# Rounding x on another engine, splitting the loads over two queues, and multiplying the first two row pairs plainly

## The chip, the cores and the metric

The kernel runs on one core of a Trainium2 chip. The metric is the device time of one execution in microseconds (us). Before the change it is 456.4 us, the median of three runs (455.51 to 456.47).

## What is computed

The inputs are `x` of 16 x 512 x 768 and `w_qkv` of 768 x 2304, both float32. The reference is one matrix product, cut into three parts:

```python
qkv = np.matmul(x, w_qkv)
q = qkv[..., :hidden]
k = qkv[..., hidden:2*hidden]
v = qkv[..., 2*hidden:]
return np.stack([q, k, v], axis=0).astype(np.float32)
```

`x` has 8192 rows. All of `x`, `w_qkv` and the output pass through the DMA queues once: 25.2 MB and 7.1 MB in, 75.5 MB out.

## The kernel before

The rows of `x` are taken in 32 pairs `p` of 2 x 128 rows. The 2304 columns of `w_qkv` are three regions: two quads `q` of 1024 columns, each of two blocks of `CB` = 512, and between them 256 remaining columns. The 768 terms of the sum are six steps of 128 (`KT`), or two halves of three (`KH`).

A pair times a quad is a 2 x 2 by 2 x 2 block product. It is done with seven block products in place of eight, and sums of blocks stand in for the eighth. Products 1 and 2 take x rounded to bf16 (tile `xb`) and w rounded to bf16 (`b11`, `b21`). Products 3 to 7 take sums of blocks of x (tile `s`, five slots) and sums of blocks of w (tiles `t1` to `t4`, and `b22`) in float32. Each product is three matmuls of 128 x 512 on PE (TensorE), at L155. `do(u, n)` issues product n of quad u and what takes its result out of PSUM: ACT (ScalarE) copies at L169, L176, L182 and L186, DVE (VectorE) adds at L173, L183 and L189. Product 1 opens PSUM tile `u.x`; products 6, 7 and 4 add into the same tile, so each of them can begin only when the ACT copy of the state before it has been read out. Products 5 and 3 share `u.y` in the same way. `rem(p)` multiplies a pair by the 256 remaining columns in bf16 (12 matmuls, L207, taken out by DVE at L212).

`two(a, b, fill, between)` interleaves two quads on PE, in the order a1, b1, a2, a6, b2, b6, a5, a7, b5, b7, a4, b4, then `rem`, then a3, b3. From pair 3 on, one call does both quads of one pair, and this is the loop: 29 calls.

Inside `two`, behind a5, stands `between()`. It calls `prep(p + 1)`: DVE transposes the next pair's x from `xin` to `xf` (L116), ACT rounds it to `xb` (L123) and copies one block into `s` (L125), and POOL (GpSimd) makes the four sums of `s` (L127 to L130). Then the load of pair p + 3 is issued. Engines work their instructions in the order of the program text; nothing is reordered.

All w loads and the x loads from pair 3 on are issued by SP (SyncE) in one queue, and so are all stores. The x loads of pairs 0 to 2 are issued by ACT. Every load of a tile is four DMAs of 32 partitions each (0 to 31, 32 to 63, 64 to 95, 96 to 127). At the start pairs 0 to 2 are prepared and their `rem` done, then w's quad 0 is rounded and summed, and the first `two` does quad 0 of pairs 0 and 1.

Of the kernel before, what the change touches and what calls it, by code (L numbers as in the profile page):

```python
# [9 lines left out]
def kernel(  # L10
# [20 lines left out]
    nc = tc.nc  # L31
    P = 128
# [5 lines left out]
    KT = K // P  # L38
    KH = KT // 2
# [45 lines left out]
    def load_block(q, h, c):  # L85
        t = big_pool.tile([P, KH, CB], fp32, name="st", tag="big")
        load_w(t, h * KH, KH, Q_OFF[q] + c * CB, CB)
        stage[q, h, c] = t

    def casts_w(q, which):  # L90
        if which == 0:
            nc.scalar.activation(b11[q][:], stage[q, 0, 0][:], ident)
            nc.scalar.activation(b21[q][:], stage[q, 1, 0][:], ident)
        else:
            nc.scalar.activation(b22[q][:], stage[q, 1, 1][:], ident)

    def sums_w(q):
        t1, t2, t3, t4 = ts[q]
        v = nc.vector
        v.tensor_tensor(t1[:], stage[q, 0, 1][:], stage[q, 0, 0][:], op=sub)  # L100
        v.tensor_tensor(t2[:], stage[q, 1, 1][:], t1[:], op=sub)
        v.tensor_tensor(t3[:], stage[q, 1, 1][:], stage[q, 0, 1][:], op=sub)
        v.tensor_tensor(t4[:], stage[q, 1, 0][:], t2[:], op=sub)

    xin, xf, xb, sr = {}, {}, {}, {}

    def load_x(p, eng):
        t = xin_pool.tile([P, 2 * P // G, KC], fp32, name="xin")
        rows = x_flat[p * 2 * P:(p + 1) * 2 * P, :].rearrange("(g b) k -> b g k", b=G)
        for i in range(4):  # L110
            eng.dma_start(t[i * G:(i + 1) * G], rows[:, :, i * KC:(i + 1) * KC])
        xin[p] = t

    def prep(p):
        t = xf_pool.tile([P, KT, 2 * P], fp32, name="xf")
# [28 lines left out]
    def product(u, n, ps, start, stop):  # L144
        b, s = xb[u.p], sr[u.p]
        t1, t2, t3, t4 = ts[u.q]
        if n == 1:
            lhs, rhs = [b[:, j, :P] for j in range(KH)], b11[u.q]
        elif n == 2:
            lhs, rhs = [b[:, KH + j, :P] for j in range(KH)], b21[u.q]  # L150
# [12 lines left out]
    def do(u, n):  # L163
        c11, c12 = u.o[:, 0, :CB], u.o[:, 0, CB:]
        c21, c22 = u.o[:, 1, :CB], u.o[:, 1, CB:]
        if n == 1:
            u.x = bank()
            product(u, 1, u.x, True, True)
            nc.scalar.activation(c11, u.x[:], ident)  # L169
        elif n == 2:  # L170
            u.z = bank()
            product(u, 2, u.z, True, True)
            nc.vector.tensor_tensor(c11, c11, u.z[:], op=add)  # L173
        elif n == 6:
            product(u, 6, u.x, False, True)
            nc.scalar.activation(c12, u.x[:], ident)  # L176
        elif n == 5:
            u.y = bank()
            product(u, 5, u.y, True, True)
        elif n == 7:  # L180
            product(u, 7, u.x, False, True)
            nc.scalar.activation(c22, u.x[:], ident)  # L182
            nc.vector.tensor_tensor(c22, c22, u.y[:], op=add)  # L183
        elif n == 4:
            product(u, 4, u.x, False, True)
            nc.scalar.activation(c21, u.x[:], ident)  # L186
# [52 lines left out]
    load_x(0, nc.scalar)  # L239
    load_x(1, nc.scalar)  # L240
    st_rem = big_pool.tile([P, KT, REM], fp32, name="st", tag="big")
    load_w(st_rem, 0, KT, R_OFF, REM)
    for h, c in ((0, 0), (1, 0), (0, 1), (1, 1)):
        load_block(0, h, c)
# [7 lines left out]
    prep(2)
    rem(2)
    casts_w(0, 1)
    sums_w(0)
    a, b = quad(0, 0), quad(1, 0)
    load_block(1, 0, 0)
    load_block(1, 1, 0)

    def rest_of_w():  # L260
        load_block(1, 0, 1)
        load_block(1, 1, 1)
        load_x(3, nc.sync)

    two(a, b, nothing, rest_of_w)
    casts_w(1, 0)
    casts_w(1, 1)
    sums_w(1)
    two(quad(2, 0), quad(0, 1), nothing, lambda: load_x(4, nc.sync))
    prep(3)  # L270
    two(quad(1, 1), quad(2, 1), nothing, lambda: load_x(5, nc.sync))

    for p in range(3, NP):
        a, b = quad(p, 0), quad(p, 1)

        def between():
            if p + 1 < NP:
                prep(p + 1)
            if p + 3 < NP:
                load_x(p + 3, nc.sync)  # L280

        two(a, b, lambda: rem(p), between)


# [28 lines left out]
```

## Time and profile before

| | |
|---|---|
| median of three runs | 456.4 us |
| the profiled execution, its own time | 455.96 us |
| its span, first to last instruction | 454.2 us |
| PE busy (matmul) | 366.0 us, 1728 matmuls |
| DVE, ACT, POOL busy | 219.1, 218.1, 126.6 us |
| moved by DMA | 108.10 MB, mean 238 GB/s |

The engines run beside each other, so the busy times don't add up to the span. 1.8 us of the time lie outside the span. Up to about 84 us the work is the start (w arrives, the first pairs are mixed), from there to 446 us the loop, and the last 8 us store what is left. Line numbers in this document's rows are those of the kernel before.

### The profile page before, as it was taken

The page shows a single profiled execution, that of the slowest core. Times are in us where ns is not written, and L with a number is a line of the kernel's source. Part 1 is how long each engine was busy: PE and PEld are TensorE (multiplying, and loading weights), DVE is VectorE, ACT ScalarE, POOL GpSimd, SP SyncE. Part 2 cuts the span into 40 slices and gives each one's busy share as a digit, 9 for nine tenths or more (in the row PEclk, how much of TensorE's full clock was granted, in tenths as well). Part 3 has the DMA queues.
Part 4 walks back from the last instruction along what each step waited for, and adds up shares of the span by engine and source line. Part 5 has one row for each costly group of instructions (what it writes and reads, how often), then busy time and mean ns, then how long its engine had stood idle before and what let it go on. Part 6 is the DMA issues. An engine that isn't in the chain of part 4 may idle for free.

```text
span 454.2 us, 5237 instructions
## 1 busy us (share of the span) xinstructions
PE 366.0 (81%) x1728; PEld 247.6 (55%) x1728; DVE 219.1 (48%) x264; ACT 218.1 (48%) x328; POOL 126.6 (28%) x132
## 2 busy tenths in 40 slices
PE   0248598888998888888898888888899888888892
PEld 0125265555665566655665556655566556665561
DVE  0328652454554455455455455445455445545542
ACT  0553535555445554554445555555544555455440
POOL 0540003332223333332222333333222333333200
PEclk9999888999999999999999999999999999999997
DMA  9988977787777777887777777788777777785555
GB/s 180 223 197 191 251 250 203 241 269 252 243 253 230 237 234 234 271 278 259 250 253 235 232 238 232 247 279 270 237 259 252 231 237 236 232 270 210 208 210 208
DMA packets 82779, 108.10 MB, mean 238 GB/s; under 512 B 5184, under 2 KB 63296, under 8 KB 82752
## 3 DMA queue, kind: packets, MB, share of 16 engines
q1 hardware_dynamic: 79488, 105.40, 74.9%
q10 hardware_dynamic: 3264, 2.36, 2.6%
q8 instruction: 14, 0.23, 0.2%
q14 instruction: 13, 0.11, 0.1%
HBM read 32.24 MB, written 75.50 MB: 237 GB/s over the span
## 4 chain that ended last, share of the span: by engine, by line
DMA 28%; PE 28%; DVE 21%; issue 12%; ACT 8%; SPq 1%; DVEq 1%; ACTq 0%
DMA out_dram<-o 19%; PE ps L155 19%; DVE xf L116 12%; PE ps L207 9%; DMA xin<-in_x_dram 5%; DVE o L189 4%; DVE orem L212 4%; DMA st<-in_w_qkv_dram 4%; ACT s L125 3%; ACT o L182 3%; ACT xb L123 1%; SPq L78 1%; DVEq L116 1%; DVE o L173 0%; ACT o L169 0%
## 5 line engine op out<-in xcount | busy, mean ns | idle before, releaser
L155 PE MATMUL ps<-t,s 128*128 128x512 f32 x768 | 210.5, 417 | 53.5 <-ACT o L182 43.9
L155 PEld LDWEIGHTS ps<-t,s 128*128 128x128 f32 x768 | 144.0, 191 | 102.4 <-ACT o L182 57.4
L127 POOL TENSOR_TENSOR s<-xf 128x384 fp32r<-128x384 f32 x32 | 32.3, 1009 | 302.9 <-DVE xf L116 302.9
L155 PE MATMUL ps<-b,xb 128*128 128x512 bf16 x384 | 96.4, 387 | 0.0
L183 DVE TENSOR_TENSOR o<-o,ps 128x512 f32<-128x512 f32 x64 | 41.5, 685 | 80.1 <-ACT o L182 80.1
L169 ACT ACTIVATE o<-ps 128x512 f32<-128x512 f32 x64 | 38.0, 596 | 84.9 <-PE ps L155 83.5
L173 DVE TENSOR_TENSOR o<-o,ps 128x512 f32<-128x512 f32 x64 | 43.9, 688 | 62.2 <-ACT o L169 38.6
L207 PE MATMUL ps<-w_rem,xb 128*128 128x256 bf16 x384 | 51.2, 287 | 26.5 <-ACT xb L123 26.5
L123 ACT ACTIVATE xb<-xf 128x1536 bf16<-128x1536 f32 x32 | 47.5, 1484 | 42.7 <-DVE xf L116 42.7
L176 ACT ACTIVATE o<-ps 128x512 f32<-128x512 f32 x64 | 38.2, 598 | 51.6 <-PE ps L155 51.6
L116 DVE STREAM_TRANSPOSE xf<-xin 128x1536 f32<-128x1536 f32 x32 | 56.8, 1774 | 10.9 <-DMA xin<-in_x_dram 10.9
L155 PEld LDWEIGHTS <-xb 128*128 128x128 bf16 x384 | 33.0, 99 | 49.1 <-issue 19.6
L207 PEld LDWEIGHTS <-xb 128*128 128x128 bf16 x384 | 36.6, 102 | 40.5 <-ACT xb L123 27.5
L212 DVE COPY orem<-ps 128x512 f32<-128x512 f32 x32 | 22.1, 692 | 68.2 <-PE ps L207 68.2
L155 PE MATMUL ps<-b,s 128*128 128x512 f32 x192 | 52.1, 406 | 0.0
L186 ACT ACTIVATE o<-ps 128x512 f32<-128x512 f32 x64 | 38.3, 598 | 20.3 <-PE ps L155 17.2
L189 DVE TENSOR_TENSOR o<-o,ps 128x512 f32<-128x512 f32 x64 | 44.0, 687 | 3.5 <-PE ps L155 3.1
L182 ACT ACTIVATE o<-ps 128x512 f32<-128x512 f32 x64 | 34.7, 586 | 7.0 <-PE ps L155 7.0
L155 PEld LDWEIGHTS ps<-b,s 128*128 128x128 f32 x192 | 33.9, 189 | 6.1
L130 POOL TENSOR_TENSOR s<-xf,s 128x384 fp32r<-128x384 f32 x32 | 32.7, 1022 | 0.0
L128 POOL TENSOR_TENSOR s<-s,xf 128x384 fp32r<-128x384 f32 x32 | 31.8, 995 | 2.5
L129 POOL TENSOR_TENSOR s<-xf 128x384 fp32r<-128x384 f32 x32 | 32.5, 1014 | 0.0
(14 smaller groups left out, 42.3 us busy)
## 6 DMA issues: line engine op xcount, KB each, us to landing
out_dram<-o SPq DMA_DIRECT2D x64, 768.0 KB, 4.8
xin<-in_x_dram SPq DMA_DIRECT2D x116, 192.0 KB, 4.0
out_dram<-o SPq DMA_DIRECT2D x64, 256.0 KB, 3.9
out_dram<-orem SPq DMA_DIRECT2D x32, 256.0 KB, 2.2
st<-in_w_qkv_dram SPq DMA_DIRECT2D x36, 192.0 KB, 6.5
xin<-in_x_dram ACTq DMA_DIRECT2D x12, 192.0 KB, 7.1
```

The lines of the kernel that those rows point to most:

```text
L116: nc.vector.transpose(t.rearrange("p j (g b) -> p g j b", b=G), xin.pop(p).rearrange("p g (j a) -> p g j a", a=G),)
L123: nc.scalar.activation(b[:], t[:], ident)
L155: nc.tensor.matmul(ps[:], lhs[j], rhs[:, j, :], start=(start and j == 0), stop=(stop and j == KH - 1), skip_group_check=True,)
L169: nc.scalar.activation(c11, u.x[:], ident)
L173: nc.vector.tensor_tensor(c11, c11, u.z[:], op=add)
L176: nc.scalar.activation(c12, u.x[:], ident)
L182: nc.scalar.activation(c22, u.x[:], ident)
L183: nc.vector.tensor_tensor(c22, c22, u.y[:], op=add)
L186: nc.scalar.activation(c21, u.x[:], ident)
L189: nc.vector.tensor_tensor(c12, c12, u.y[:], op=add)
L207: nc.tensor.matmul(ps[:, r, :], xb[p][:, j, r * P:(r + 1) * P], w_rem[:, j, :], start=(j == 0), stop=(j == KT - 1), skip_group_check=True,)
L212: nc.vector.tensor_copy(out=o[:], in_=ps[:])
```

## The change

- Rounding: x is rounded to bf16 on POOL (`round_x`), and POOL also copies the block into `s`; ACT no longer does either. In the loop, transpose, rounding and sums of pair p + 1 are issued behind b1 of pair p (`early`), not behind a5.
- The result of `rem` is taken out by ACT, not by DVE, and `rem` stands between a4 and b4.
- Loads: of the four DMAs of a tile, those to partitions 0 to 63 are issued by SP, those to 64 to 127 by a second engine, in the order 0, 2, 1, 3. The second engine is POOL for w and for x of pairs 0 to 3, ACT for x from pair 4 on. In the loop the load of pair p + 2 is issued behind b1 of pair p.
- Pairs 0 and 1 are multiplied plainly in bf16, one block of 512 columns at a time as w arrives (`direct`: 24 matmuls for each block and both pairs), 96 matmuls in place of 84. DVE rounds w for it. Then pairs 2 and 3 go through two calls of `two` (quad 0, then quad 1), and the loop begins with pair 4: 30 calls in all.
- w's sums are made one by one between this work; those of quad 1 go into the buffers that w's quad 0 was staged in.

```diff
-    def load_w(dst, j0, nj, off, cols):
-        for i in range(4):
+    def load_w(dst, j0, nj, off, cols, other):
+        for i in (0, 2, 1, 3):
             k0 = i * KC + j0 * G
-            nc.sync.dma_start(
+            eng = nc.sync if i < 2 else other
+            eng.dma_start(
...
-    def load_x(p, eng):
+    def load_x(p, other):
...
-        for i in range(4):
+        for i in (0, 2, 1, 3):
+            eng = nc.sync if i < 2 else other
             eng.dma_start(t[i * G:(i + 1) * G], rows[:, :, i * KC:(i + 1) * KC])
...
-    def prep(p):
+    def transpose(p):
...
+    def round_x(p):
+        xb[p] = xb_pool.tile([P, KT, 2 * P], bf16, name="xb")
+        nc.gpsimd.tensor_copy(out=xb[p][:], in_=xf[p][:])
+
+    def sums_x(p):
...
-        nc.scalar.activation(b[:], t[:], ident)
         s = s_pool.tile([P, 5, KH, P], f32r, name="s")
-        nc.scalar.activation(s[:, 0], a22, ident)
...
+        g.tensor_copy(out=s[:, 0], in_=a22)
...
-        nc.vector.tensor_copy(out=o[:], in_=ps[:])
+        nc.scalar.activation(o[:], ps[:], ident)
...
+    def direct(p, c, o, w):
+        for r in range(2):
+            ps = bank()
+            for j in range(KT):
+                nc.tensor.matmul(
+                    ps[:], xb[p][:, j, r * P:(r + 1) * P], w[:, j, :],
+                    start=(j == 0), stop=(j == KT - 1),
+                )
+            nc.scalar.activation(o[:, r, c * CB:(c + 1) * CB], ps[:], ident)
...
-    def two(a, b, fill, between):
+    def two(a, b, fill, early, mid):
         do(a, 1)
         do(b, 1)
+        early()
         do(a, 2)
         do(a, 6)
         do(b, 2)
         do(b, 6)
         do(a, 5)
-        between()
         do(a, 7)
         do(b, 5)
         do(b, 7)
+        mid()
         do(a, 4)
+        fill()
         do(b, 4)
-        fill()
         do(a, 3)
...
+    w = casts(0, 0)
+    direct(0, 0, o0[0].o, w)
+    direct(1, 0, o0[1].o, w)
+    transpose(2)
+    round_x(2)
+    sums_x(2)
+    load_x(3, gp)
+    w = casts(0, 1)
+    direct(0, 1, o0[0].o, w)
...
+    two(quad(2, 0), quad(3, 0), lambda: rem(2), nothing, nothing)
+    def ahead():
+        transpose(4)
+        round_x(4)
+        sums_x(4)
+    two(quad(2, 1), quad(3, 1), lambda: rem(3), lambda: load_x(5, ac), ahead)
+    for p in range(4, NP):
+        def early():
+            if p + 1 < NP:
+                transpose(p + 1)
+                round_x(p + 1)
+                sums_x(p + 1)
+            if p + 2 < NP:
+                load_x(p + 2, ac)
+        two(quad(p, 0), quad(p, 1), lambda: rem(p), early, nothing)
```

On ACT, one call of the loop before reads as follows; L169, L176, L182 and L186 are the copies behind products 1, 6, 7 and 4, each for quads a and b.

```order
L169 ACTIVATE o<-ps 128x512 x2
L176 ACTIVATE o<-ps 128x512 x2
L123 ACTIVATE xb<-xf 128x1536
L125 ACTIVATE s<-xf 128x384
L182 ACTIVATE o<-ps 128x512 x2
L186 ACTIVATE o<-ps 128x512 x2
```

After the change the same call on ACT is this, with the copies now at L179, L186, L192 and L196, the remaining columns at L222, and two x loads at L115.

```order
L179 ACTIVATE o<-ps 128x512 x2
L115 DMA xin<-in_x_dram 32x8x192 x2
L186 ACTIVATE o<-ps 128x512 x2
L192 ACTIVATE o<-ps 128x512 x2
L196 ACTIVATE o<-ps 128x512
L222 ACTIVATE orem<-ps 128x512
L196 ACTIVATE o<-ps 128x512
```

The two instructions on x between the copies are gone from ACT; two DMA issues and the copy of the remaining columns have come.

On POOL the program after the change begins with these loads (`str` is the remaining columns of w, `st` a staged half block of w), ahead of the first two roundings of x; POOL issued no DMA before.

```order
L115 DMA xin<-in_x_dram 32x8x192 x2
L82 DMA str<-in_w_qkv_dram 32x6x256 x2
L115 DMA xin<-in_x_dram 32x8x192 x2
L82 DMA st_111<-in_w_qkv_dram 32x3x512 x2
L82 DMA st_116<-in_w_qkv_dram 32x3x512 x2
L82 DMA st_121<-in_w_qkv_dram 32x3x512 x2
L82 DMA st_126<-in_w_qkv_dram 32x3x512 x2
L128 CAST xb<-xf 128x1536 x2
L115 DMA xin<-in_x_dram 32x8x192 x2
```

In the loop POOL's share of one pair is now these six instructions; before it was the four sums alone.

```order
L128 CAST xb<-xf 128x1536
L136 TENSOR_TENSOR s<-xf 128x384
L137 TENSOR_TENSOR s<-s,xf 128x384
L138 TENSOR_TENSOR s<-xf 128x384
L139 CAST s<-xf 128x384
L140 TENSOR_TENSOR s<-xf,s 128x384
```

The rounding stands ahead of the sums of the same pair.

## Rows read from the trace of the kernel before

**Rows 1.** The page's head and its first part.

```profile
span 454.2 us, 5237 instructions
PE 366.0 (81%) x1728; PEld 247.6 (55%) x1728; DVE 219.1 (48%) x264; ACT 218.1 (48%) x328; POOL 126.6 (28%) x132
```

**Rows 2.** Windows: busy us (and count) by engine, granted clock, DMA share, GB/s.

```profile
54.00:83.80 29.80, 26.46 (x95) 17.21 (x96) 14.57 (x19) 12.62 (x22) 3.91 (x4) 0.84 0.80 247
83.80:185.15 101.35, 88.87 (x433) 60.74 (x432) 51.32 (x65) 51.60 (x80) 31.64 (x32) 1.00 0.77 246
```

**Rows 3.** Waits from 83.8 to 426.3 us: total us, times, longest.

```profile
POOL s L127 <- DVE xf L116: 238.9, 27, 14.0
...
PE ps L155 <- ACT o L182: 42.3, 27, 1.6
```

**Rows 4.** The chain that ended last, inside one loop call: start, us, what.

```profile
248.59 1.78 DVE xf L116
...
251.84 0.51 ACT s L125
252.35 0.49 ACT o L182
```

**Rows 5.** Timeline of the same call and the next one's beginning.

```profile
244.42 2.12 PE L155 MATMUL ps<-b,xb 128*128 128x512 bf16 x9
246.19 1.04 PE L155 MATMUL ps<-t,s 128*128 128x512 f32 x3
247.54 3.78 PE L155 MATMUL ps<-t,s 128*128 128x512 f32 x15
252.89 1.66 PE L155 MATMUL ps<-t,s 128*128 128x512 f32 x6 [1.57 <-ACT o L182]
255.63 1.64 PE L155 MATMUL ps<-b,s 128*128 128x512 f32 x6
257.11 1.25 PE L155 MATMUL ps<-b,xb 128*128 128x512 bf16 x5
...
258.01 1.25 ACT L169 ACTIVATE o<-ps 128x512 f32<-128x512 f32 x2 [2.83 <-PE ps L155]
```

**Rows 6.** Timeline of the last call on PE, its first and last rows.

```profile
434.78 2.12 PE L155 MATMUL ps<-b,xb 128*128 128x512 bf16 x9
...
444.41 1.64 PE L155 MATMUL ps<-b,s 128*128 128x512 f32 x6
```

**Rows 7.** The page's groups of x's preparation: busy us, mean ns, idle before.

```profile
L127 POOL TENSOR_TENSOR s<-xf 128x384 fp32r<-128x384 f32 x32 | 32.3, 1009 | 302.9 <-DVE xf L116 302.9
...
L123 ACT ACTIVATE xb<-xf 128x1536 bf16<-128x1536 f32 x32 | 47.5, 1484 | 42.7 <-DVE xf L116 42.7
...
L116 DVE STREAM_TRANSPOSE xf<-xin 128x1536 f32<-128x1536 f32 x32 | 56.8, 1774 | 10.9 <-DMA xin<-in_x_dram 10.9
```

**Rows 8.** Timeline of the start, and the page's time to landing of w.

```profile
0.73 10.38 ACTq L111 DMA_DIRECT2D xin<-in_x_dram  x8
...
15.48 2.74 PE L207 MATMUL ps<-w_rem,xb 128*128 128x256 bf16 x12 [15.48 <-ACT xb L123]
...
52.29 1.48 ACT L95 ACTIVATE b<-st 128x1536 fp32r<-128x1536 f32 x1 [3.18 <-DMA st<-in_w_qkv_dram]
...
st<-in_w_qkv_dram SPq DMA_DIRECT2D x36, 192.0 KB, 6.5
```

**Rows 9.** Windows of the start while only loads run, columns as in rows 2.

```profile
4.00:6.00 2.00, 0.00 (x0) 0.00 (x0) 0.00 (x0) 0.00 (x0) 0.00 (x0) 1.00 1.13 206
38.00:40.00 2.00, 0.93 (x4) 0.60 (x5) 2.00 (x2) 0.00 (x0) 0.00 (x0) 1.00 1.06 241
```

**Rows 10.** Windows of 1 us inside one loop call, columns as in rows 2.

```profile
245.40:246.40 1.00, 1.00 (x7) 0.51 (x5) 0.00 (x0) 0.95 (x2) 0.00 (x0) 1.00 1.06 393
...
253.40:254.40 1.00, 1.00 (x6) 0.59 (x6) 0.75 (x2) 0.52 (x1) 1.00 (x2) 1.00 1.12 224
...
256.40:257.40 1.00, 1.00 (x6) 0.56 (x5) 0.99 (x3) 0.00 (x0) 0.00 (x0) 1.00 0.00 0
```

More of the change, by code (lines that the diff above doesn't have):

```diff
@@ L83, with load_blocks, sum_w @@
     stage = {}
[L85 to L97, printed above, removed]
-        t1, t2, t3, t4 = ts[q]
[L99 to L103, printed above, removed]
+    def load_blocks(q, c, other):
+        for h in range(2):
+            if q == 0:
+                t = tq_pool.tile([P, KH, CB], fp32, name="st0", tag="tq")
+            else:
+                t = big_pool.tile([P, KH, CB], fp32, name="st1", tag="big")
+            load_w(t, h * KH, KH, Q_OFF[q] + c * CB, CB, other)
+            stage[q, h, c] = t
+    def sum_w(q, n):
+        t1, t2, t3, t4 = ts[q]
+        o, in0, in1 = {
+            1: (t1, stage[q, 0, 1], stage[q, 0, 0]),
+            2: (t2, stage[q, 1, 1], t1),
+            3: (t3, stage[q, 1, 1], stage[q, 0, 1]),
+            4: (t4, stage[q, 1, 0], t2),
+        }[n]
+        nc.vector.tensor_tensor(o[:], in0[:], in1[:], op=sub)
     xin, xf, xb, sr = {}, {}, {}, {}
-    def load_x(p, eng):
+    def load_x(p, other):
         t = xin_pool.tile([P, 2 * P // G, KC], fp32, name="xin")
         rows = x_flat[p * 2 * P:(p + 1) * 2 * P, :].rearrange("(g b) k -> b g k", b=G)
-        for i in range(4):
+        for i in (0, 2, 1, 3):
+            eng = nc.sync if i < 2 else other
             eng.dma_start(t[i * G:(i + 1) * G], rows[:, :, i * KC:(i + 1) * KC])
         xin[p] = t
-    def prep(p):
+    def transpose(p):
         t = xf_pool.tile([P, KT, 2 * P], fp32, name="xf")
@@ L142, in quad, with product @@
         return u
-    def product(u, n, ps, start, stop):
-        b, s = xb[u.p], sr[u.p]
+    def product(u, n, ps, start):
         t1, t2, t3, t4 = ts[u.q]
[L147 to L150, printed above, removed]
-        else:
-            k, rhs = {3: (4, b22[u.q]), 4: (0, t4), 5: (1, t1), 6: (2, t2), 7: (3, t3)}[n]
-            lhs = [s[:, k, j, :] for j in range(KH)]
+        if n <= 2:
+            h = (n - 1) * KH
+            lhs = [xb[u.p][:, h + j, :P] for j in range(KH)]
+            rhs = [b1[u.q][:, h + j, :] for j in range(KH)]
+        else:
+            k, t = {3: (4, b22[u.q]), 4: (0, t4), 5: (1, t1), 6: (2, t2), 7: (3, t3)}[n]
+            lhs = [sr[u.p][:, k, j, :] for j in range(KH)]
+            rhs = [t[:, j, :] for j in range(KH)]
         for j in range(KH):
             nc.tensor.matmul(
-                ps[:], lhs[j], rhs[:, j, :],
-                start=(start and j == 0), stop=(stop and j == KH - 1), skip_group_check=True,
+                ps[:], lhs[j], rhs[j],
+                start=(start and j == 0), stop=(j == KH - 1), skip_group_check=True,
             )
@@ L167, in do @@
             u.x = bank()
-            product(u, 1, u.x, True, True)
+            product(u, 1, u.x, True)
             nc.scalar.activation(c11, u.x[:], ident)
@@ L236 @@
     nothing = lambda: None
[L239 to L244, printed above, removed]
-    nc.scalar.activation(w_rem[:], st_rem[:], ident)
-    prep(0)
-    load_x(2, nc.scalar)
+    gp, ac = nc.gpsimd, nc.scalar
+    load_x(0, gp)
+    st_rem = big_pool.tile([P, KT, REM], fp32, name="str", tag="big")
+    load_w(st_rem, 0, KT, R_OFF, REM, gp)
@@ L248 @@
+    load_x(1, gp)
+    load_blocks(0, 0, gp)
+    load_blocks(0, 1, gp)
+    transpose(0)
+    round_x(0)
+    nc.scalar.activation(w_rem[:], st_rem[:], ident)
+    transpose(1)
+    round_x(1)
+    load_x(2, gp)
+    o0 = [quad(p, 0) for p in range(2)]
+    load_blocks(1, 0, gp)
+    load_blocks(1, 1, gp)
+    o1 = [quad(p, 1) for p in range(2)]
     rem(0)
-    casts_w(0, 0)
-    prep(1)
     rem(1)
[L252 to L276, printed above, removed]
-            if p + 1 < NP:
[L278 to L282, printed above, removed]
+    def casts(q, c):
+        w = b1[q] if c == 0 else bt_pool.tile([P, KT, CB], bf16, name="bt")
+        for h in range(2):
+            nc.vector.tensor_copy(out=w[:, h * KH:(h + 1) * KH, :], in_=stage[q, h, c][:])
+        return w
@@ new lines @@
+    w = casts(0, 0)
[7 more added lines that the diff above has]
+    direct(0, 1, o0[0].o, w)
+    store_quad(o0[0])
+    direct(1, 1, o0[1].o, w)
+    store_quad(o0[1])
+    nc.scalar.activation(b22[0][:], stage[0, 1, 1][:], ident)
+    sum_w(0, 1)
+    sum_w(0, 2)
+    w = casts(1, 0)
+    direct(0, 0, o1[0].o, w)
+    direct(1, 0, o1[1].o, w)
+    transpose(3)
+    round_x(3)
+    sums_x(3)
@@ new lines @@
+    sum_w(0, 3)
+    sum_w(0, 4)
+    w = casts(1, 1)
+    direct(0, 1, o1[0].o, w)
+    store_quad(o1[0])
+    direct(1, 1, o1[1].o, w)
+    store_quad(o1[1])
+    nc.scalar.activation(b22[1][:], stage[1, 1, 1][:], ident)
+    ts[1] = [tq_pool.tile([P, KH, CB], f32r, name=f"t{n + 1}_1", tag="tq") for n in range(4)]
+    for n in range(1, 5):
+        sum_w(1, n)
+    load_x(4, ac)
+    two(quad(2, 0), quad(3, 0), lambda: rem(2), nothing, nothing)
[3 more added lines that the diff above has]
+        sums_x(4)
```

28 lines of the change are left out of this document (15 added, 13 removed).

## The prediction

> **What bounds the kernel now.** I read the page's head first, then the windows by stage, the waits, the chain that ended last, and the timeline of one loop call; the start last. The head says that PE is the busiest engine, 366.0 of 454.2 us, and that no other reaches half [rows 1]. So PE should set the pace, and the question is what keeps it from working. In the loop PE is busy 88.87 of 101.35 us at granted clock 1.00 [rows 2]: 12.5 us are lost over eight calls. The waits give the whole of that loss one name: PE at L155 waited 27 times for ACT at L182, 42.3 us in all, 1.57 us each [rows 3].
>
> The chain shows what is late. Inside a call it goes from DVE's transpose (1.78 us) over ACT's rounding to ACT's copy into `s` (0.51), then to the copy at L182 that releases PE [rows 4]. ACT works in program order: the two preparation instructions of the next pair stand ahead of the copy that product a4 needs, and the first of them waits for the transpose. A call starts at 244.42 and the next at 257.11: 12.69 us. Without the 1.57 us wait it is 11.12 us of pure matmul flow [rows 5].
>
> The last call proves that number. It prepares nothing, and on PE it begins at 434.78; its last group of six begins at 444.41 [rows 6]. In a usual call the same group begins at 255.63, 1.48 us before the next call at 257.11 [rows 5]. 434.78 to 444.41 plus 1.48 is 11.11 us, with no wait. So 11.11 to 11.12 us is what PE needs for a call.
>
> At the start PE has little to do. The last staged block of w is waited for until 52.29 us [rows 8], and up to 83.8 us PE works in part at a mean clock of 0.84, between the two levels of 1.2 and 2.4 GHz [rows 2].
>
> **The change part by part: the loop.** The rounding (1.48 us) and the block copy (0.51 us) leave ACT, and the copy behind product 7 no longer stands behind the transpose. What is late next? I go through one call with T as its start.
> - ACT's copies behind 1a and 1b end at T + 2.15 (258.01 + 1.25, against 257.11) [rows 5]. Now two DMA issues follow, then the copy behind a6, which a7 needs at T + 4.6 (247.54 + two groups of 3.78 / 5, against 244.42). The slack for the issues is 4.6 - 2.15 - 0.6 = 1.9 us. An issue cost 10.38 / 8 = 1.30 us when eight were issued in a row at the start [rows 8]; alone it can only be less. Two issues thus cost at most 2.6 us; I take them as hidden and keep the other end as a rival.
> - `rem` between a4 and b4 gives b4 1.2 us more until it needs its copy; it costs PE nothing. The copy of `rem` moves from DVE to ACT, 0.6 us, which has 1.99 us less to do.
> - DVE: the transpose now stands ahead of the adds behind 2a and 2b, so these are up to 1.8 us later. PE needs the first DVE result only for a3, at T + 9.6. Hidden.
> - POOL: before, it waited 14 us at a time for the transpose and was otherwise free [rows 3]. It now has per pair four sums of 1.01 us [rows 7], a copy of 384 and the rounding of 1536 elements. The trace has no such rounding on POOL. From below it is ACT's 1.48 us for the same shape, from above four times the two-input sum of 384 elements, 4.04 us [rows 7]. A rounding reads one input and not two, so I take half the upper end, 2.0 us, which is also near the lower row. POOL then has 4.0 + 0.5 (ACT's price for that copy [rows 4]) + 2.0 = 6.5 us of work per call of 11.1. The transpose ends at about T + 2.5, `xb` is ready at T + 4.5, `s` at T + 9.0, and the next call starts at T + 11.1. Even at 4.04 us it is hidden.
> - DMA: each call moves 3.15 MB (0.79 of x, 2.36 of output). Inside a call the queue runs at 393 GB/s while stores are in it, at 224 when only loads of 32 partitions are left, and at 0 for the last 2 us [rows 10]. So it needs some 10.5 us of 12.7, still below 11.1. x(p + 2) must land within about 11 us of its issue and has 5 us more before PE feels it, since transpose, rounding and sums have that much slack.
>
> So a call should take PE's 11.12 us. I add 0.05 us for small waits. With 30 calls: 333.6 + 1.5 us. One seam costs: `ahead` transposes pair 4 only behind b7 of the second call, at about T + 8.5; plus 1.8 and 2.0 us `xb` is ready at T + 12.3, 1.2 us after the third call wants it. Together 336.3 us.
>
> **The start.** PE cannot begin before POOL has rounded x of pair 0, and POOL first issues 14 loads [order rows of the change]. The price of a POOL issue is not in the trace. From below it is nothing; then the landing of x decides, which released the first transpose at 10.9 us [rows 7], and the rounding begins 1.8 us later, at 12.7 (some 2 us sooner if the split speeds the load). From above I add POOL's dearest row to the full-queue issue, 1.01 + 1.30 = 2.3 us: it begins at 33 us. I take the row of loads issued in a run, 1.30 us [rows 8]: 0.7 + 14 x 1.30 = 18.9 us. The rounding makes it 20.9. Then PE does `rem` of two pairs at its slow level, 2 x 2.74 us [rows 8], and 96 matmuls. Nine bf16 matmuls took from 244.42 to 246.19, 0.197 us each [rows 5]: 18.9 us, plus 3 for the part at the lower clock. PE reaches the first call of `two` at 20.9 + 5.5 + 18.9 + 3 = 48.3 us.
>
> Does w arrive in time? Up to its last block 9.44 MB are loaded (7.08 of w, three pairs of x). With one queue, or two that walk through the partitions in step, the loads ran at 206 to 241 GB/s with the DMA engines fully taken [rows 9]; a mix with stores reached 393 [rows 10]. At 393 it is all there at 26 us; POOL's second batch of ten issues then decides: 18.9 + 4 + 13 = 36 us, plus 3 to 6.5 to land [rows 8], plus two roundings of w (1.48 each) and the last 24 matmuls (4.7): 47 to 50. It agrees with 48.3, which I keep.
>
> A rule speaks against the split. The Trainium skill, page "DMA: Bandwidth & Descriptors", section "Rules for kernel authors", says that two transfers to disjoint partition halves serialize, since both use the same 16 engines, and that spreading DMAs over issuing engines does not help bandwidth. No row of the trace has the two halves in flight side by side, so it neither agrees nor differs. By the rule the loads stay at the rate of rows 9, and that is the first rival.
>
> **The sum.** 48.3 + 336.3 + the tail. The tail is 454.2 - (444.41 + 1.64) = 8.1 us [rows 1, 6]; nothing in it changes. Span 392.7; with 1.8 us outside it 394.5. The profiled execution (455.96) stood 0.4 below the median, so the median should be about 394.9. I say 394.5. Against before, 1.57 x 27 = 42 us come from the loop, the rest from the start.
>
> **The rivals.**
> 1. The loads serialize at 228 GB/s, the middle of what rows 9 bracket. 9.44 MB take 41.4 us, with the first 2 us empty 43.4; roundings 3.0 and 24 matmuls 4.7 give 51.1 us instead of 48.3: 397.5 us. For it: the full share at 206 to 241. Against: 393 with the same engines.
> 2. POOL's issues or its roundings are dear (2.3 us each): the start takes 33 + 4 + 27.4 = 64 us, the time is about 411. For it: POOL is new as a load issuer. The Trainium skill, page "SBUF — State Buffer", section "Who interferes with whom", adds that DVE copies in a two-port mode lock POOL out, descriptor writing included; no run here shows that yet.
> 3. ACT's two DMA issues cost the full 1.30 us each. The a6 copy then ends at T + 2.15 + 2.6 + 0.6 = 5.35, 0.75 us after a7 wants it, in 28 calls: 21 us, so 415.
> 4. The slow side: POOL becomes the bound of the loop. Its work per pair is 4.04 + 0.5 + the rounding. Slower than before begins where the call is longer by (456.4 - 394.5) / 30 = 2.06 us, at 13.2 us: a rounding of 8.7 us or more. At 10 us the call is 14.5 and the time 495. For it: no POOL rounding in the trace, and POOL now sits between DVE and PE. Against: that is 5.7 ns per element, and POOL's two-input sum takes 2.6.
> 5. Another wait takes the place of L182 and half the gain in the loop goes (11.9 us a call): 394.5 + 23 = 418.
>
> **How the numbers follow.** Forecast 0.64, rival 1 0.12, rival 2 0.08, rival 3 0.07, rival 4 0.04, rival 5 0.05. The forecast's own range is 384 (the rounding of pair 0 begins at 10 to 11 us, no small waits) to 402. Rivals 1 and 2 lie up to 411, so 384 to 411 holds about 8 in 10. What the measurement can tell is 0.2%, 0.9 us: faster 0.95 (all but rival 4 and a little), same 0.01, slower 0.04.
>
> **What would show it.** Right: PE's wait for the copy behind product 7 is gone from the waits, calls follow each other at 11.1 to 11.2 us, PE is busy over 95% in the loop, and the first float32 product begins at 46 to 51 us. Wrong in the loop: a new name at the top of PE's waits (POOL's `xb`, or the copy behind a6 behind ACT's DMA issues). Wrong at the start: POOL's queue still issuing past 40 us, or GB/s staying under 245 while only loads run. A time above 420 would mean that PE is not what sets the loop.

## The result, and the profile after

The changed kernel takes 403.27 us, the median of four runs (402.73 to 404.48), against 455.95 for the kernel before on the same chip: a ratio of 0.885, with a 95% interval of 0.8824 to 0.8875. The forecast was 394.5, so it is 8.8 us short. The profiled execution took 403.43 us, with a span of 401.6 and so again 1.8 us outside it; the forecast's span was 392.7. Rows below carry each kernel's own line numbers. After the change L165 is the block products, L217 `rem`, L230 the plain products of `direct`, L285 DVE's rounding of w for them, L106 the sums of w, L120 the transpose, L128 POOL's rounding of x, L136 to L140 the rest of POOL's share.

The page's head and first part, which answer to [rows 1]:

```profile
span 401.6 us, 5114 instructions
PE 355.2 (88%) x1740; PEld 243.2 (61%) x1740; DVE 204.9 (51%) x228; ACT 177.5 (44%) x292; POOL 206.2 (51%) x212
```

ACT lost 40.6 us of work and POOL won 79.6, its DMA issues among them. PE has 12 matmuls more and yet 10.8 us less busy time. Most of that is small waits that its modelled spans had held inside them: the run e7 below, with the same matmuls and only `rem` moved back, shows 364.8 us.

Two long windows of the loop (columns as in [rows 2]: length, busy by engine, clock, DMA share, GB/s):

```profile
90.46:201.00 110.54, 110.54 (x551) 77.92 (x552) 58.67 (x72) 55.03 (x92) 62.60 (x65) 1.00 0.89 288
201.00:382.00 181.00, 181.00 (x908) 129.01 (x907) 94.36 (x118) 90.33 (x151) 99.23 (x102) 1.00 0.88 288
```

PE is busy in every microsecond; before it was 88.87 of 101.35. The waits of PE over the whole execution (total us, times, longest) say the same, and answer to [rows 3]:

```profile
PE ps L230 <- DVE bt L285: 19.6, 4, 10.7
PE ps L217 <- POOL xb L128: 16.4, 1, 16.4
PE ps L230 <- DVE b L285: 1.0, 3, 0.4
PE ps L165 <- POOL xb L128: 0.7, 1, 0.7
PE ps L165 <- ACT o L179: 0.6, 1, 0.6
```

The 42.3 us at the copy behind product 7 are gone and no name has taken their place in the loop: the only loop entry is 0.7 us, once, for `xb`, at the seam that the prediction priced at 1.2. The two large names belong to the start. One call of the loop on the timeline (start, us, what; compare [rows 5]):

```profile
209.52 2.12 PE L165 MATMUL ps<-b,xb 128*128 128x512 bf16 x9
...
211.19 1.65 ACTq L115 DMA_DIRECT2D xin<-in_x_dram  x2
...
212.16 1.46 POOL L128 CAST xb<-xf 128x1536 bf16<-128x1536 f32 x1 [4.89 <-DVE xf L120]
...
212.65 4.44 PE L165 MATMUL ps<-t,s 128*128 128x512 f32 x18
...
216.93 1.48 PE L217 MATMUL ps<-w_rem,xb 128*128 128x256 bf16 x12
217.07 1.00 POOL L140 TENSOR_TENSOR s<-xf,s 128x384 fp32r<-128x384 f32 x1
...
218.17 0.95 PE L165 MATMUL ps<-t,s 128*128 128x512 f32 x3
...
220.33 1.90 PE L165 MATMUL ps<-b,xb 128*128 128x512 bf16 x8
```

A call is 220.33 - 209.52 = 10.81 us, less than the 11.12 that the prediction read as PE's own need. POOL's rounding costs 1.46 us, ACT's two DMA issues 1.65 together, and POOL is done 2.3 us before the next call. All of that is hidden.

The start went otherwise. PE's timeline (the bracket is the idle time just before and what ended it):

```profile
16.36 4.30 PE L217 MATMUL ps<-w_rem,xb 128*128 128x256 bf16 x24 [16.36 <-POOL xb L128]
...
21.70 4.69 PE L230 MATMUL ps<-b,xb 128*128 128x512 bf16 x21 [0.40 <-DVE b L285]
34.42 1.44 PE L230 MATMUL ps<-bt,xb 128*128 128x512 bf16 x3 [8.03 <-DVE bt L285]
...
59.73 1.46 PE L230 MATMUL ps<-bt,xb 128*128 128x512 bf16 x3 [10.70 <-DVE bt L285]
...
67.12 2.10 PE L165 MATMUL ps<-b,xb 128*128 128x512 bf16 x9
```

PE began at 16.36 us, earlier than the forecast 20.9, but reached the first call of `two` at 67.1 and not at 48.3. Two stretches, 8.03 and 10.70 us, were spent waiting for DVE to round the second block of each quad of w. DVE's own timeline shows what it did in that time:

```profile
31.75 1.78 DVE L120 STREAM_TRANSPOSE xf<-xin 128x1536 f32<-128x1536 f32 x1 [10.10 <-DMA xin<-in_x_dram]
33.45 3.06 DVE L285 CAST bt<-st 128x1536 bf16<-128x1536 f32 x2
...
51.65 1.78 DVE L120 STREAM_TRANSPOSE xf<-xin 128x1536 f32<-128x1536 f32 x1 [7.36 <-DMA xin<-in_x_dram]
53.35 1.72 DVE L106 TENSOR_TENSOR t<-st,st 128x1536 fp32r<-128x1536 f32 x1
54.99 3.02 DVE L106 TENSOR_TENSOR t<-st,t 128x1536 fp32r<-128x1536 f32 x1
57.93 3.41 DVE L285 CAST bt<-st 128x1536 bf16<-128x1536 f32 x2
```

DVE waited 10.10 and 7.36 us for x of pairs 2 and 3, which nobody needed yet, while the roundings that PE wanted stood behind those transposes in its queue. And x of pair 3 came late because its load was late, as POOL's timeline shows:

```profile
43.44 1.70 POOL L140 TENSOR_TENSOR s<-xf,s 128x384 fp32r<-128x384 f32 x1
45.09 1.18 POOL L115 DMA_DIRECT2D xin<-in_x_dram  x2
```

POOL issued its half of that load behind the sums of pair 2. From 52 to 66 us nothing was in flight any more. PE had stood still since 49 us, and from 54 to 62 us its granted clock was 0.50, the lower of its two levels (1.2 GHz); one window of that stretch (columns as above):

```profile
56.00:58.00 2.00, 0.00 (x0) 0.00 (x0) 2.00 (x2) 0.00 (x0) 2.00 (x2) 0.50 0.00 0
```

So the sum is: start 67.1 where 48.3 was forecast (+18.8), the 30 calls with their seams 401.6 - 67.1 - 8.2 = 326.3 where 336.3 was (-10.0), and the tail 8.2 where 8.1 was; +8.9 in the span.

### The profile page after: what moved, and what is told of

It is laid out like the page before. It is cut to its first block, busy times and chain, and to the rows that moved or that the text cites. A ratio compares the mean times of both kernels' runs of the same rounds, so it can differ in the third digit from the quotient of the medians.

```text
span 401.6 us, 5114 instructions
## 1 busy us (share of the span) xinstructions
PE 355.2 (88%) x1740; PEld 243.2 (61%) x1740; DVE 204.9 (51%) x228; ACT 177.5 (44%) x292; POOL 206.2 (51%) x212
## 4 chain that ended last, share of the span: by engine, by line
PE 79%; DMA 8%; DVE 4%; issue 3%; POOL 2%; SPq 1%; ACT 0%; ACTq 0%; DVEq 0%; POOLq 0%
PE ps L165 68%; PE ps L217 10%; DMA xin<-in_x_dram 5%; DMA st<-in_w_qkv_dram 3%; PE ps L230 1%; DVE t L106 1%; DVE xf L120 1%; POOL xb L128 1%; DVE bt L285 1%; POOL s L137 1%; SPq L115 0%; POOL s L136 0%; SPq L82 0%; DVE o L199 0%; DVE b L285 0%
## 5 line engine op out<-in xcount | busy, mean ns | idle before, releaser
L165 PE MATMUL ps<-t,s 128*128 128x512 f32 x720 | 192.9, 410 | 0.6 <-ACT o L179 0.6
L165 PEld LDWEIGHTS ps<-t,s 128*128 128x128 f32 x720 | 133.1, 188 | 31.9 <-ACT o L179 1.1
L128 POOL CAST xb<-xf 128x1536 bf16<-128x1536 f32 x32 | 48.8, 1528 | 160.9 <-DVE xf L120 160.9
L165 PE MATMUL ps<-b,xb 128*128 128x512 bf16 x360 | 88.1, 381 | 0.7 <-POOL xb L128 0.7
L193 DVE TENSOR_TENSOR o<-o,ps 128x512 f32<-128x512 f32 x60 | 41.3, 688 | 78.2 <-ACT o L192 78.2
L120 DVE STREAM_TRANSPOSE xf<-xin 128x1536 f32<-128x1536 f32 x32 | 56.7, 1773 | 30.8 <-DMA xin<-in_x_dram 30.6
L199 DVE TENSOR_TENSOR o<-o,ps 128x512 f32<-128x512 f32 x60 | 41.0, 687 | 60.7 <-PE ps L165 60.7
L217 PE MATMUL ps<-w_rem,xb 128*128 128x256 bf16 x384 | 48.8, 279 | 16.4 <-POOL xb L128 16.4
L165 PEld LDWEIGHTS <-xb 128*128 128x128 bf16 x360 | 30.4, 98 | 45.2 <-issue 15.5
L192 ACT ACTIVATE o<-ps 128x512 f32<-128x512 f32 x60 | 35.9, 598 | 45.7 <-PE ps L165 45.7
L186 ACT ACTIVATE o<-ps 128x512 f32<-128x512 f32 x60 | 35.9, 599 | 44.9 <-DVE o L183 26.5
L179 ACT ACTIVATE o<-ps 128x512 f32<-128x512 f32 x60 | 35.8, 598 | 44.0 <-PE ps L165 41.0
L217 PEld LDWEIGHTS <-xb 128*128 128x128 bf16 x384 | 35.8, 100 | 28.6 <-POOL xb L128 16.4
L183 DVE TENSOR_TENSOR o<-o,ps 128x512 f32<-128x512 f32 x60 | 40.2, 671 | 16.0 <-issue 8.7
L165 PE MATMUL ps<-b,s 128*128 128x512 f32 x180 | 46.0, 391 | 0.0
L165 PEld LDWEIGHTS ps<-b,s 128*128 128x128 f32 x180 | 33.8, 188 | 7.7
L196 ACT ACTIVATE o<-ps 128x512 f32<-128x512 f32 x60 | 35.9, 598 | 4.2
L136 POOL TENSOR_TENSOR s<-xf 128x384 fp32r<-128x384 f32 x30 | 32.6, 1085 | 0.0
L230 PE MATMUL ps<-bt,xb 128*128 128x512 bf16 x48 | 15.2, 480 | 19.6 <-DVE bt L285 19.6
L140 POOL TENSOR_TENSOR s<-xf,s 128x384 fp32r<-128x384 f32 x30 | 32.3, 1076 | 0.0
```

What stands on the lines that cost most here:

```text
L120: nc.vector.transpose(t.rearrange("p j (g b) -> p g j b", b=G), xin.pop(p).rearrange("p g (j a) -> p g j a", a=G),)
L128: nc.gpsimd.tensor_copy(out=xb[p][:], in_=xf[p][:])
L165: nc.tensor.matmul(ps[:], lhs[j], rhs[j], start=(start and j == 0), stop=(j == KH - 1), skip_group_check=True,)
L217: nc.tensor.matmul(ps[:, r, :], xb[p][:, j, r * P:(r + 1) * P], w_rem[:, j, :], start=(j == 0), stop=(j == KT - 1), skip_group_check=True,)
```

## The experiments

Letters in the expectations: A is the order on DVE's queue (roundings of w behind transposes that wait for x) and the late load of pair 3; B is POOL as the issuer of half the loads; C is DVE and POOL slowing each other down; D is `rem` between a4 and b4; the others are said where they come up.

**The order at the start: e1_casts_first, e2_x3_early.** The first puts the roundings ahead of the transposes:

```diff
+    w = casts(0, 1)
     transpose(2)
     round_x(2)
     sums_x(2)
     load_x(3, gp)
-    w = casts(0, 1)
...
+    w = casts(1, 1)
     transpose(3)
...
-    w = casts(1, 1)
```

> The changed kernel with DVE's order at the start altered: the roundings of w's block 1 of quad 0 stand ahead of the transpose of pair 2, and those of block 1 of quad 1 ahead of the transpose of pair 3. Theory A (the first call of the loop came 18.6 us later than forecast because DVE, working in order, held these roundings behind transposes that wait for x: PE idle 8.0 and 10.7 us): most of the idle goes, but pair 3's x still lands at 51 us and the first call needs it, so the first call begins near 55 instead of 67 us and the time is 390 to 396. Theory B (POOL is a slow issuer of loads, so w itself is late): no change, 402 to 404. Theory C (DVE and POOL slow each other at the start): at most 3 us, 400 to 403.

Measured: 393.61 us (393.53 to 394.2), ratio 0.8643 [0.8629, 0.8657]; 9.7 us less than the changed kernel. PE's waits for DVE's roundings fell from 20.6 to 9.5 us. The first call began at 52.8 us, but then waited 1.67 for `xb` and 2.13 for `s` of pair 3, whose x was still late. The second kernel moves that load as well:

```diff
     load_blocks(1, 1, gp)
+    load_x(3, gp)
...
     sums_x(2)
-    load_x(3, gp)
```

> As the run before, and the load of pair 3's x is issued right behind w's last block, ahead of POOL's sums of pair 2 and of the first stores. Theory A: pair 3 lands near 43 us and not at 51.6, the first call begins at 49 to 52 us, the time is 386 to 391. Theory B: 400 or more. Theory C: 398 to 402.

Measured: 387.68 us (387.04 to 388.17), ratio 0.8509 [0.8494, 0.8525], 5.9 us less again. PE at the start of this kernel:

```profile
25.47 5.34 PE L230 MATMUL ps<-bt,xb 128*128 128x512 bf16 x24
39.13 1.46 PE L230 MATMUL ps<-b,xb 128*128 128x512 bf16 x3 [8.31 <-DVE b L286]
...
46.09 5.34 PE L230 MATMUL ps<-bt,xb 128*128 128x512 bf16 x24
51.27 2.11 PE L165 MATMUL ps<-b,xb 128*128 128x512 bf16 x9
```

Both second blocks (`bt`) now follow without a wait. Not one matmul, byte or rounding was taken out, so 15.6 us of the start were order alone: 9.7 us the order on DVE, 5.9 us the place of one load. One wait of 8.31 is left, for the first block of quad 1 (L286 is the same rounding): DVE has a transpose and two sums of w ahead of it.

**DVE and POOL beside each other: e8_w_casts_on_act, e10_casts_act_ahead.** In the first 70 us POOL's sums take about twice what they take in the loop (us busy, mean ns; the loop's row above has 1.00 us, [rows 7] 1.01):

```profile
L137 POOL TENSOR_TENSOR s<-s,xf 128x384 fp32r<-128x384 f32 x2 | 4.0, 1990 | 0.2
...
L138 POOL TENSOR_TENSOR s<-xf 128x384 fp32r<-128x384 f32 x2 | 4.2, 2107 | 0.0
```

and DVE's sums of w, 1.75 us in the trace of before, are longer too:

```profile
L106 DVE TENSOR_TENSOR t<-st,st 128x1536 fp32r<-128x1536 f32 x4 | 9.3, 2336 | 0.0
L106 DVE TENSOR_TENSOR t<-st,t 128x1536 fp32r<-128x1536 f32 x4 | 9.1, 2284 | 0.1
```

Row by row the two engines take turns. From 52 to 62 us no DMA is in flight and ACT does nothing, so only DVE and POOL can hold each other up (PE starts again at 59.7). POOL's first two rows there:

```profile
53.49 2.90 POOL L128 CAST xb<-xf 128x1536 bf16<-128x1536 f32 x1 [7.22 <-DVE xf L120]
56.36 2.50 POOL L136 TENSOR_TENSOR s<-xf 128x384 fp32r<-128x384 f32 x1
```

DVE's sum of 53.35 ends at 55.07 and POOL's rounding 1.32 us later, at 56.39; DVE's next sum ends 1.62 us after that, at 58.01, and POOL's sum 0.85 us after it, at 58.86. Counted from the end of the other engine's instruction, each takes about what it takes alone (1.46, 1.75 and 1.01 us).

The first experiment takes the roundings of w off DVE, at the same place in the program:

```diff
-            nc.vector.tensor_copy(out=w[:, h * KH:(h + 1) * KH, :], in_=stage[q, h, c][:])
+            nc.scalar.activation(w[:, h * KH:(h + 1) * KH, :], stage[q, h, c][:], ident)
```

> The changed kernel with the eight roundings of w at the start on ACT instead of DVE, order in the text unchanged. Theory A: ACT does not wait for x, so the first idle stretch of PE (8.0 us) and the second (10.7) shrink, down to the landing of pair 3 at 51 us: first call near 55 us, time 390 to 396. Theory C: POOL's sums at the start, now 1.6 to 2.5 us each, fall to the loop's 1.02, since DVE's copies are gone, and POOL's share gains some us. Theory B: no change.

Measured: 396.29 us (395.07 to 398.12), ratio 0.8703 [0.8673, 0.8732], first call at 59.4. A's mechanism shows: on ACT nothing stands ahead that waits for x, and PE's longest wait for a rounding falls from 10.70 to 3.43 us. Its numbers don't quite: the first call was expected near 55 us, and the time is just above 390 to 396. C is not decided by it. Of POOL's sums L136 rose from 2.05 to 2.46 us and the others fell only to 1.69 to 1.76,

```profile
L136 POOL TENSOR_TENSOR s<-xf 128x384 fp32r<-128x384 f32 x2 | 4.9, 2456 | 0.0
...
L138 POOL TENSOR_TENSOR s<-xf 128x384 fp32r<-128x384 f32 x2 | 3.5, 1750 | 0.0
```

since DVE's sums of w, 2.13 to 2.59 us in this kernel, are still beside them. What the turns cost in time no run separates, since the next one changes the order too. The second starts from e2 and has ACT round each block a block ahead:

```diff
     w = casts(0, 0)
+    w01 = casts(0, 1)
     direct(0, 0, o0[0].o, w)
     direct(1, 0, o0[1].o, w)
...
+    w = casts(1, 0)
-    direct(0, 1, o0[0].o, w)
+    direct(0, 1, o0[0].o, w01)
...
+    w11 = casts(1, 1)
```

> The reordered start with two queues (387.7 us) and the roundings of w on ACT, each a block ahead of its use. Theory C' (what is left of PE's 8.3 us idle at 31 to 39 us is DVE: transpose of pair 2, two sums of w and two roundings in a row, each slowed beside POOL): the idle falls to 2 to 4 us, the first call begins at 45 to 48 us, time 382 to 385. If the idle is the landing of w, at most 1 us is gained: 387 to 389.

Measured: 386.14 us (384.27 to 386.3), ratio 0.847 [0.8442, 0.8497], the best version of all. Against e2 it is 1.5 us; the two intervals just touch, so that step is likely but not certain. It fell between the two expectations. PE:

```profile
37.16 0.81 PE L230 MATMUL ps<-b,xb 128*128 128x512 bf16 x3 [2.37 <-ACT b L286]
...
43.39 5.34 PE L230 MATMUL ps<-bt,xb 128*128 128x512 bf16 x24
48.57 2.11 PE L165 MATMUL ps<-b,xb 128*128 128x512 bf16 x9
```

The wait of 8.31 is down to 2.37, and the first call begins at 48.6 us, where the prediction had it (48.3).

**The split of the loads: e4_one_queue, e9_same_half, e3_act_queue, e11_x3_early_one_queue.** The first gives the start's loads to SP alone, in the order 0 to 3; the second keeps two issuers, but SP takes DMAs 0 and 2 and POOL 1 and 3, so that both halves of the partitions are in each queue; the third has ACT issue what POOL issued:

```diff
# e4_one_queue
-        for i in (0, 2, 1, 3):
+        for i in ((0, 1, 2, 3) if other is nc.sync else (0, 2, 1, 3)):
...
-    gp, ac = nc.gpsimd, nc.scalar
+    gp, ac = nc.sync, nc.scalar
# e9_same_half
-        for i in (0, 2, 1, 3):
+        for i in ((0, 2, 1, 3) if other is nc.scalar else (0, 1, 2, 3)):
...
-            eng = nc.sync if i < 2 else other
+            eng = nc.sync if (i < 2 if other is nc.scalar else i % 2 == 0) else other
# e3_act_queue
-    gp, ac = nc.gpsimd, nc.scalar
+    gp, ac = nc.scalar, nc.scalar
```

> The changed kernel with all loads of the start in one queue (SP), four DMAs in the order 0, 1, 2, 3 as in the kernel before; the loop is unchanged. If the split by halves raised the load rate (changed kernel: 258 to 313 GB/s between 4 and 20 us, before 206 to 241), the rate falls back to 205 to 245 and the first call comes 4 to 10 us later: 406 to 413. If halves serialize anyway, as the Trainium skill's rule has it (page DMA: Bandwidth & Descriptors, section Rules for kernel authors), the rate does not change and the time is 402 to 405.

> The changed kernel with the loads of the start still over SP and POOL, but so that both work on the same half of the partitions at a time: SP takes quarters 0 and 2, POOL 1 and 3. If it is the half that matters, the rate falls to 205 to 245 GB/s between 4 and 20 us and the time to 406 to 413; if two queues are what matters, it stays at 258 to 313 GB/s and at 402 to 405 us.

> The changed kernel with the second half of every load at the start issued by ACT in place of POOL. Theory B (POOL as issuer is what makes the start late): 8 us or more faster, 395 or less. Theory A: the transposes of pairs 2 and 3 wait for x just as before, 400 to 407 (ACT then has loads in front of its copies, which may cost a few us).

Measured: e4 400.68 us (398.74 to 402.5), ratio 0.8801 [0.876, 0.8841]; e9 406.32 (404.86 to 407.01), 0.8921 [0.889, 0.8953]; e3 398.29 (397.61 to 398.88), 0.8748 [0.8731, 0.8764]. The window from 4 to 20 us, in which only loads run (columns as above), of the changed kernel, of e9, of e4 and of e3:

```profile
4.00:20.00 16.00, 3.64 (x20) 2.68 (x21) 4.86 (x3) 3.36 (x3) 10.41 (x16) 1.00 1.04 281
```

```profile
4.00:20.00 16.00, 3.92 (x19) 2.80 (x20) 4.99 (x3) 3.36 (x3) 10.69 (x16) 1.00 1.05 268
```

```profile
4.00:20.00 16.00, 5.63 (x25) 3.62 (x26) 4.52 (x3) 3.50 (x4) 2.93 (x2) 1.00 1.07 239
```

```profile
4.00:20.00 16.00, 0.00 (x0) 0.10 (x1) 5.48 (x4) 1.33 (x2) 2.93 (x2) 1.00 1.09 253
```

With SP and POOL as issuers the loads run at 281 GB/s, with SP alone at 239, so this split raises the rate by 18%. With mixed halves it is 268, and from 20 to 40 us 277 against the changed kernel's 266, so over both windows the halves make no difference to the rate (SP alone gives 239 here and 228 in e11, so a step of 13 is no more than two runs differ by). Yet e9 takes 3 us longer, clear of the noise; x of pairs 2 and 3 is transposed 1.5 and 1.1 us later there. So e9 has the rate of its second expectation and the time of its first. A second issuer as such doesn't do it either: with ACT in POOL's place the rate is 253, and from 20 to 40 us 235, where e4 has 242. What raised the rate is POOL as the second issuer; why its loads run faster beside SP's is not shown. e4's time fits neither of its expectations: it is 2.6 us lower than the changed kernel's, not higher (the two intervals overlap a little). What differs stands in e4's DVE row: x of pair 3, whose load no longer stands behind POOL's sums, is transposed at 47.38 and not at 51.65.

```profile
47.38 1.78 DVE L120 STREAM_TRANSPOSE xf<-xin 128x1536 f32<-128x1536 f32 x1 [4.83 <-DMA xin<-in_x_dram]
```

e3, between its two expectations, gained 5 us, likely by the same route (transposed at 46.13), though its first `rem` had to wait until 21.5 us, for ACT's rounding of w behind ACT's own issues. It changes too much at once to price POOL's issues. The last one settles what the split is worth when the order is right: e2 with one queue.

> The reordered start (roundings of w ahead of the transposes, x of pair 3 loaded behind w; 387.7 us with two queues) with all start loads in SP's one queue, quarters in the order 0 to 3. Theory F (the split raises the rate from 240 to about 290 GB/s, and this pays once nothing else is late): w and x of 10.2 MB land 6 to 8 us later, the first call begins at 54 to 59 instead of 51.3 us, time 391 to 396. Rival (POOL's issuing and the order of loads cost what the rate gains, as in the unordered start, where one queue was 2.6 us faster): 385 to 389.

Measured: 392.68 us (392.43 to 393.31), ratio 0.8625 [0.8604, 0.8645], against 0.8509 [0.8494, 0.8525] for e2, with 228 against 282 GB/s from 4 to 20 us. So the split pays 5.0 us there, and in the changed kernel it was buried under the order. The first call begins at 51.8 us, hardly later than in e2 and earlier than expected; the loss comes inside it, where PE waits 4.6 us in all for pair 3's `xb` and `s` and for an add on DVE.

**The loop: e6_before_pool_round, e5_round_on_act, e7_rem_after_b4, e12_before_loop_edits.** e6 is the kernel before with one edit, the rounding and the block copy on POOL at their old place:

```diff
-        nc.scalar.activation(b[:], t[:], ident)
+        nc.gpsimd.tensor_copy(out=b[:], in_=t[:])
...
-        nc.scalar.activation(s[:, 0], a22, ident)
...
+        g.tensor_copy(out=s[:, 0], in_=a22)
```

> The kernel before with one edit: the rounding of x and the block copy on POOL, at their old place behind a5. If the engine alone takes the wait away, calls go from 12.69 to 10.8 to 11.1 us (b4 may still wait 0.3 for its copy, since the remaining columns stay behind b4): 27 to 29 calls give 43 to 55 us, the time is 402 to 414. If the place matters too, POOL's sums come too late for the next call (ready near T + 12 against a call of 11) and calls stay above 11.5 us: 420 or more.

Measured: 402.38 us (401.44 to 403.78), ratio 0.8841 [0.8808, 0.8875]. This one edit gives what the whole change gives. Calls follow at 11.11 us where they took 12.69:

```profile
238.35 1.89 PE L155 MATMUL ps<-b,xb 128*128 128x512 bf16 x8
...
249.46 1.89 PE L155 MATMUL ps<-b,xb 128*128 128x512 bf16 x8
```

So 28 x 1.58 = 44 us come from the loop. The other 9 come in the main from the start: pair 3's call begins at 71.4 us, before at 79.6. e5 is the opposite, the changed kernel with rounding and block copy back on ACT, but at the early place:

```diff
-        nc.gpsimd.tensor_copy(out=xb[p][:], in_=xf[p][:])
+        nc.scalar.activation(xb[p][:], xf[p][:], ident)
...
-        g.tensor_copy(out=s[:, 0], in_=a22)
+        nc.scalar.activation(s[:, 0], a22, ident)
```

> The changed kernel with the rounding of x and the block copy back on ACT, but at their new, early place in the loop. If the place alone made the gain, calls stay at 10.8 us and the time at 401 to 405. If the engine matters, ACT's copy behind a6 waits for the transpose (ends at T + 2.6) plus 1.48 and 0.51 us and two issues, ends near T + 5.6 to 6.5 and holds a7 (wanted at T + 4.3) by 1.3 to 2.2 us: calls of 12.1 to 13.0 us, time 440 to 465.

Measured: 417.75 us (417.11 to 418.69), ratio 0.9183 [0.915, 0.9217], which is neither of the two expectations. Among PE's waits stands

```profile
PE ps L165 <- ACT o L186: 8.9, 26, 0.9
```

The copy behind a6 now comes behind the rounding, but late by 0.3 to 0.5 us in PE's rows and not by 1.57; calls are about 11.4 us (384.73 to 396.13). So the early place alone takes away most of the loop's wait, and the engine takes away the rest. e7 tests why a call is 10.81 and not 11.12: the changed kernel with `rem` back behind b4.

```diff
-        fill()
         do(b, 4)
+        fill()
```

> The changed kernel with the remaining columns back behind b4 instead of between a4 and b4. Theory D (in the changed kernel calls take 10.81 us and not the 11.12 forecast because b4 no longer waits for ACT's copy of its tile; before, that wait was hidden in PE's modelled ends): calls go back to 11.1 us, 28 to 30 calls give 8 to 9 us, the time is 410 to 413. Theory E (the place of the tiles in memory or the other engines' load made the matmuls quicker): calls stay at 10.8 us, time 402 to 405.

Measured: 411.21 us (409.96 to 411.77), ratio 0.902 [0.8992, 0.9049]; calls are 11.12 again (379.33 to 390.45). Weight loads of that kernel, inside one call:

```profile
237.93 4.07 PEld L165 LDWEIGHTS ps<-t,s 128*128 128x128 f32 x18
242.43 0.53 PEld L165 LDWEIGHTS ps<-t,s 128*128 128x128 f32 x3 [0.43 <-ACT o L192]
```

The first weights of b4 wait 0.43 us for ACT's copy behind b7. PE's matmul row shows no wait there, since its ends are modelled. With `rem` ahead of b4 the wait is gone. The last kernel is the one before with three edits of the loop (POOL's rounding, `rem` between, its copy on ACT); x's preparation stays behind a5, and start and loads are the old ones:

> The kernel before with the rounding on POOL (as in the run that gave 402.4), the remaining columns between a4 and b4, and their copy on ACT; start, loads and pairs 0 to 2 as before. Theory A (the changed start loses time against the old one, because DVE holds w's roundings behind late x): 29 calls at 10.8 instead of 11.1 us give 392 to 395, so that the changed kernel's start costs 8 to 11 us. If the changed start is a gain or neutral, this kernel is at 403 or more.

Measured: 394.75 us (394.29 to 395.63), ratio 0.867 [0.8648, 0.8693]. Its calls take 10.81 us too, so the early place of x's preparation adds nothing once POOL does the rounding. It beats the whole change by 8.5 us: pair 4's call begins at 82.29 us there, at 90.46 in the changed kernel and at 73.09 in e10. So the changed start cost 8.5 us as it was ordered, and saves 8.6 when it is ordered well.

## Why the prediction came out as it did

- The time lies in the range, in part by luck. 403.27 us is above the forecast's own range (384 to 402), in the part up to 411 that was added for rivals 1 and 2, and neither of these is what happened. The start took 18.8 us more than forecast and the calls 10.0 less; with the forecast's calls the time would have been about 413, outside the range. Two signs of being right came (no wait behind product 7, PE busy all through the loop), two did not (calls of 10.81 us, the first float32 product at 69.8), and one sign of being wrong did: POOL still issued a load at 45.09.
- What bounds the loop: right. PE's flow set it, the 1.57 us went, nothing came instead; e6 shows that ACT's two instructions were the cause.
- "11.11 to 11.12 us is what PE needs for a call": this term was mis-sized. It measured 10.81. The last call of before, from which it was read, held a weight wait of b4 inside modelled matmul spans [rows 6]. The trace of before has it in its weight loads:

```profile
442.37 0.53 PEld L155 LDWEIGHTS ps<-t,s 128*128 128x128 f32 x3 [0.43 <-ACT o L182]
```

Of `rem` between a4 and b4 it was said that "it costs PE nothing", but it gave back 0.3 us a call, 7.9 us by e7. With it about half of the miss at the start was hidden.
- POOL's rounding: 1.46 us against 2.0 chosen, at the low bound of 1.48. Seam 0.65 against 1.2, tail 8.2 against 8.1.
- POOL's issues: 0.57 us each and not 1.30, 8.0 us for the first 14; another 5.6 us went in gaps that the trace ends with the landing of earlier loads. The rounding was done at 16.4 and not at 20.9.
- The step that failed: "PE does `rem` of two pairs ... and 96 matmuls", priced as one flow after its first input. Its own work was about right (30.1 us between waits, against 27.4: `rem` 4.3 against 5.5, the 96 matmuls 25.8 against 21.9, of which the 3 us for the lower clock stood on no row). What was left out is 20.6 us of waits. I asked when w lands and added "two roundings", but not what stands ahead of those roundings on DVE. The program has the transposes of pairs 2 and 3 there, each waiting for a load. e1 shows that this order cost 9.7 us, and e2 that the late load of pair 3 cost 5.9 more.
- The load check ("47 to 50, it agrees") was right about arrival, but not by its terms: the loads end at about 40 us (239 GB/s from 38 to 40 us, 33 from 40 to 42), where it had 39 to 42.5, but POOL issues its last load of w at 27.4 and not at 36. With that arrival and a better order e10 starts its first call at 48.6.
- Rival 1: the loads did not stay at the old rate. The Trainium skill's rule ("DMA: Bandwidth & Descriptors", "Rules for kernel authors") that more issuers don't help bandwidth agrees with e3 (SP and ACT, 253 and 235 GB/s in the two windows, against 239 and 242 for SP alone) and not with the changed kernel (SP and POOL, 281 and 266). Two slips stand in this rival: the middle of 206 and 241 is 223.5 and not 228, and 51.1 us in place of 48.3 gives 397.3 and not 397.5.
- Rival 2 named POOL, and a start of 64 us, close to the 67 that came; but its mechanism was the price of an issue, and the runs show order instead. A part of it was real: POOL's half of pair 3's load stood behind POOL's sums. The Trainium skill's other rule ("SBUF — State Buffer", "Who interferes with whom"), that one of DVE and POOL is locked out while the other's instruction runs, agrees with the turns that rows L128, L136 and L106 take at the start, 1.3 to 1.5 us beyond their own time in each row. No run shows it for the writing of descriptors: POOL's issues took 0.57 to 0.66 us in the mean of each group, and the gaps between them end with landings.
- Rivals 3 to 5: ACT's issues took 0.83 us each and stayed hidden; POOL's rounding was far below 8.7 us; no wait took the old one's place.

## What to carry to other kernels

When an engine works in program order, price a new start by its queue: for each instruction that the busiest engine waits for, list what stands ahead of it on its engine and what each of those waits for. Here work for later pairs put ahead of work for now, and a load put behind sums, cost three times what the split of the loads could pay (15.6 against 5.0 us). And when a change has several parts, run the one that removes the measured wait alone: here it gave as much as the whole change, and of the rest the place of `rem` gave about 8 us and the start took 8.5.

## What the runs showed of the hardware

- POOL as a second issuer beside SP raised the load rate from 239 to 281 GB/s (268 with the halves mixed), in DMAs of 32 partitions; ACT in its place gave 253, and 235 in the next 20 us (SP alone 242).
- POOL rounds 128x1536 from float32 to bf16 in 1.46 us, what ACT takes (1.48); beside DVE's roundings and sums of w the same rounding took 2.10 and 2.90 us in single rows.
- DVE's sums of w and POOL's sums of x slow each other, from 1.75 to 2.3 us and from 1.0 to 2.0 us in the mean; row by row each ends about its own time after the other's instruction has ended.
- A wait of PE's weight load (0.43 us) can cost 0.3 us a call without showing in a matmul row.
